# Reordering the fill products and slowing an inverse's steps in a one-core encoder layer, with the norm sum taken by 128 columns

## The chip, the core and the metric

The kernel runs on one core of a Trainium2 chip. The metric is the device time of one launch in microseconds (us), the median of several runs. One more run, taken with the hardware profiler on, gives the trace that is read here. TensorE is called PE in the profile's rows, its weight loads PEld, VectorE DVE, ScalarE ACT, GpSimd POOL; SP issues most DMAs.

## The reference

One encoder layer on two sequences of 256 tokens (T = 512 token columns in all, D = 1024), in float32:

```
h = RMSNorm(x)
proj = h @ w_in            # q|k|v of 8 heads, decay and beta logits, gates z, latents, 3 x 1024 merge gates
A: conv + SiLU on q, k, v; l2norm of q and k; gated delta rule in both directions; RMSNorm; * silu(z_gdn)
B: latent attention with rotary keys, 8 heads; * silu(z_mla)
C: cross-attention into 256 memory tokens, 4 heads; * silu(z_mem)
y = x + (gate0*(A @ w_br_gdn) + gate1*(B @ w_br_mla) + gate2*(C @ w_br_mem)) @ w_out, then RMSNorm
```

Branch A, per head and direction: within a chunk, a unit lower-triangular matrix (identity plus masked k k^T with decay and beta) is inverted; the inverse is applied to values and keys, a state is carried from chunk to chunk, and the output is normed over its 128 channels: `o * rsqrt(mean(o*o) + eps)`.

## The kernel before, in words

Every large product is made of 24 matmuls of 128x512: the weight block of 128 output rows and the activations are each split into a rounded part and a rest, and three of the four part products are summed over eight blocks of 128 (`gemm`, L257 to L278). A product needs its weights: a load that SP issues (L229), rounded by ScalarE (L241), the rest taken by VectorE (L244). It accumulates in a PSUM bank of the tag gm, of which `middle` has four, and holds it until its result is read out.

The work has three stages. `front` does the memory branch, the latents and the eight heads of branch B, with some products of branch A and of the gates put between. `middle` does the delta rule of branch A, head by head, and fills TensorE's free time with the remaining products. `back` does the last products and the output.

In `middle` the order of TensorE's instructions is written by a planner, `weave` (L1623). It keeps a clock of its own, `now`. Six chains are generators that yield a pair (cost on TensorE, time until the next step is due). When no chain's step is due, the planner takes one matmul from the fill list `self.fill` and moves its clock on by 0.217 us, which is the cost of a matmul that `gemm` yields. The chains are:

- `preps` (L1560): the block inverses of head group 0, then of group 1 (`gdn_prep`). Its 31 inverse steps (L900 to L906) are two VectorE instructions each, a multiply into `tm` (L903) and an add into `tt` (L905), on sizes 31 to 256 elements a partition; each step needs the one before. After them a reordering copy on GpSimd (L908), two transposes on VectorE (L911, L913) and seven copies on GpSimd (L922). For group 1 these copies wait until head 3 is in `self.started` (its `yp` products have been issued and 7.5 us of the planner's clock have passed). When they are done plus 4 us, heads 4 to 7 may be solved.
- `heads_in` (`gdn_in`): one head after the other, decay masks, the products `kk` of its keys and queries (L1010, two pairs a head, each of the four products three matmuls in a gm bank of its own), read out by VectorE into `ne` (L1020). A head begins when it is at most two ahead of the outputs and its values have been stored (`self.v_done`). 18 us of the planner's clock lie between its begin and its first `kk`.
- `lane(0)` and `lane(1)` (`gdn_solve`): the even and the odd heads, each a sequence of small products (`p`, `yp`, `u`, `xs`, `us`, `x`).
- `heads_out` (`gdn_out`): the output products `o`, the gate, and the norm's sum `so` (L1182), which adds, over the four blocks of 32 partitions, the sums of squares left there by a VectorE transpose and reduction; then a power on GpSimd (L1185), a transpose (L1188) and a store of the row `d_n`.
- `heads_norm` (`gdn_norm`): reads that row back and makes the head's operand `xg` of the branch product.

VectorE, ScalarE, GpSimd and SP are in-order queues; the order within them is set when the kernel is built, by a priority and a modelled readiness, not by hand. Chains get an earlier priority than fill (the inverse chain 100, a head's solve 2000).

The fill list (`plan`, L1425 to L1466) holds products of these kinds. A query or value product (`qkv_tile`) is read out by ScalarE into `cz` (L767), which frees its bank; then comes the convolution, four VectorE instructions (L776) and a last one (L778); `v_tokens` transposes a head's values on VectorE (L801) and stores them by four DMAs of SP. A gate product (`gate_tile`) is read out by one ScalarE instruction (L1248) and stored by one DMA of SP (L1254). A `z_tile` product is read out by ScalarE (L1220) and then by VectorE (L1221), and only the second frees its bank; those of branch C (here ze) also multiply by the attention output on GpSimd. `cz`, the gates' and the z tiles share two buffers of the tag ct. After the listed products come four loads of the branch C operands, eight branch C products with their gates, eight branch B products (bm, which need all operands `xa`), and the branch A products begun with the heads that are ready (`bg_begin`).

The norm's sum uses the constant `i32` (128 rows by 32 columns, a one where row mod 32 equals the column) as weights. In the constant tile the columns of `anc`, `trf`, `trb` and `i32` lie next to each other, 32 each.

Of the kernel before, what the change touches and what calls it, by code (L numbers as in the profile page):

```python
# [10 lines left out]
ALU = mybir.AluOpType  # L11
# [6 lines left out]
EPS = 1e-6  # L18
# [49 lines left out]
def _consts():  # L68
    t = np.arange(P)
    b = t // 32  # L70
    same = b[:, None] == b[None, :]
    le = t[:, None] <= t[None, :]
    ge = t[:, None] >= t[None, :]
    z, o = np.zeros((P, P)), np.ones((P, P))
    a8 = np.arange(8)
    anc = np.zeros((P, 2, 2, 8))
    for tb in range(2):
        tg = tb * P + t
        anc[:, 0, tb] = tg[:, None] >= 32 * a8[None]
        anc[:, 1, tb] = tg[:, None] < 32 * (a8[None] + 1)  # L80
    i32 = np.arange(32)
    m = (t % 32)[:, None]
    parts = [
        ("id", np.eye(P)),
        ("anc", anc.reshape(P, 32)),
        ("trf", m <= i32), ("trb", m >= i32), ("i32", m == i32),
        ("ngf", np.where(i32 > m, 0.0, NEG)), ("ngb", np.where(i32 < m, 0.0, NEG)),
        ("one", np.ones((P, 1))), ("hf", np.full((P, 4), -0.5)), ("ph", np.full((P, 16), 0.5)),
    ]
    off, c = {}, 0  # L90
    for n, a in parts:
        off[n] = (c, c + a.shape[1])
        c += a.shape[1]
    sums = [same, same & le, same & ge, z, le, o, o, ge, z]
    return (np.concatenate([a.astype(np.float32) for _, a in parts], 1), off,
            np.concatenate([a.astype(np.float32) for a in sums], 1))


_CST, _OFF, _SUM = _consts()
# [82 lines left out]
class Layer:  # L182
# [36 lines left out]
    def c(self, n):  # L219
        lo, hi = _OFF[n]  # L220
        return self.cst[:, lo:hi]
# [587 lines left out]
    def gdn_prep(self, g):  # L809
# [4 lines left out]
        nc, c = self.nc, self.c  # L814
# [85 lines left out]
        for i in range(31):  # L900
            n, m = 31 - i, i + 1
            t3 = tms[:, i % 4, 0:n * m].rearrange("p (a b) -> p a b", a=n)
            nc.vector.tensor_tensor(t3, xx[:, m:, i:i + 1].to_broadcast([P, n, m]),  # L903
                                    tt[:, i:i + 1, 0:m].to_broadcast([P, n, m]), op=ALU.mult)
            nc.vector.tensor_tensor(tt[:, m:, 0:m], tt[:, m:, 0:m], t3, op=ALU.add)  # L905
            yield 0.0, 1.2  # L906
        ts = self.pb.tile([P, 32, 32], F32, tag="blk", bufs=3, name=f"ts{g}")
        nc.gpsimd.tensor_copy(out=ts, in_=tt.rearrange("p r c -> p c r"))  # L908
        yield 0.0, 7.0
# [234 lines left out]
    def gdn_out(self, hh):  # L1144

        nc, pg, c = self.nc, self.pg, self.c
        par, kq = hh % 2, self.kq[hh]
        (na, es, vt), ub = self.hd[hh], self.ub[hh]

        op = self.ps_ms(par, f"o{hh}")  # L1150
        o3 = op.rearrange("p (s t) -> p s t", s=2)
        for s in range(2):
            n = 0
            for d in range(2):
                for cp in range(2):
                    if cp == 0:
                        out, rhs = o3[:, s], es[:, d, s, 0:256]
                    else:
                        lo = 128 * (1 - d)
                        out, rhs = o3[:, s, lo:lo + 128], es[:, d, s, 256:384]  # L1160
                    nc.tensor.matmul(out, ub[:, d, s, cp], rhs, start=n == 0, stop=n == 3)  # L1161
                    n += 1
            yield 1.3, 0.0

        og = self.ta(f"og{hh}")
        nc.sync.dma_start(og, self.d_z[:, hh])
        self.out = hh + 1
        nc.vector.scalar_tensor_tensor(og, op, self.gg, og, ALU.mult, ALU.mult)
        sq = self.tb(f"sq{hh}")
        nc.scalar.activation(sq, op, AF.Square)  # L1170
        with self.behind():
            nc.scalar.activation(kq[:, :, 1], kq[:, :, 1], AF.Square, scale=0.064)
        s3 = sq.rearrange("p (s t) -> p s t", s=2)
        nc.vector.tensor_tensor(s3, s3, kq[:, :, 1], op=ALU.add)
        st = self.tb(f"st{hh}")
        red = self.rr[:, 16:32]
        with self.behind():
            nc.vector.transpose(out=st, in_=sq)
            nc.vector.tensor_reduce(red, st.rearrange("p (j i) -> p j i", i=32), axis=AX.X, op=ALU.add)
        yield 0.0, 13 if hh == 7 else 12  # L1180
        ssp = self.ps_ms(par, f"so{hh}")
        nc.tensor.matmul(ssp[0:32, 0:16], c("i32"), red, start=True, stop=True)  # L1182
        rr = self.rr[0:32, 0:16]
        nc.vector.tensor_scalar(rr, ssp[0:32, 0:16], 1.0 / 128, 128 * EPS * EPS, ALU.mult, ALU.add)  # L1184
        nc.gpsimd.tensor_tensor(rr, rr, c("hf")[0:32, 0:1].to_broadcast([32, 16]), op=ALU.pow)  # L1185
        yield 0.25, 2.0 if hh == 7 else 4.0
        with self.behind():
            nc.vector.transpose(out=self.rt[0:32], in_=self.rr[0:32])  # L1188
        nc.sync.dma_start(self.d_n[hh].rearrange("(j i) -> j i", i=32), self.rt[0:16])
        self.og[hh] = og, self.now + 8.0  # L1190

    def keep(self, i):
# [244 lines left out]
    def plan(self):  # L1437

        self.kq, self.xg, self.merged = {}, {}, [None] * 8
        self.cn, self.now, self.prep_on = {}, 0.0, False  # L1440
        self.v_done, self.k_done, self.z_done = set(), set(), set()
        self.fill = []
        def qv(h):
            return [(self.qkv_tile, h, 1), (self.qkv_tile, h, 2)]

        k = [(self.qkv_tile, h, 0) for h in range(8)]
        vt = [(self.v_tokens, h) for h in range(8)]
        self.xe_split, self.begun, self.k_at, self.prep_steps = False, {}, 0.0, 0
        self.xe, self.xa, self.xa_at, self.xa_raw, A = [], [None] * 8, {}, {}, self.A
        xa = [(f, n) for n in range(5) for f in (self.load_xa, self.split_xa)]  # L1450
        g = [(self.gate_tile, j, d) for j in (0, 1) for d in range(8)]
        z = [(self.z_tile, C_ZG + h, self.d_z[:, h]) for h in range(8)]
        ze = [(self.z_tile, C_ZE + h, self.d_xm[:, h], self.d_om[:, h]) for h in range(4)]
        be = [(self.branch_mem, d) for d in range(8)]
        xe = [(self.load_xe, f) for f in range(4)]

        self.fill += g[0:1] + k[0:1] + g[1:2] + k[1:4] + qv(0) + vt[0:1] + qv(1) + vt[1:2] + g[2:3] + qv(2) + vt[2:3] + g[3:4] + qv(3) + vt[3:4] + g[4:6]

        self.fill += k[4:5] + g[6:7] + k[5:6] + g[7:8] + k[6:7] + g[8:9] + k[7:8] + z[0:1] + g[9:10] + z[1:2]
        self.fill += qv(4) + g[10:11] + z[2:3] + ze[0:1] + vt[4:5] + qv(5) + g[11:12] + z[3:4] + ze[1:2] + vt[5:6] + qv(6)  # L1460
        self.fill += g[12:13] + z[4:5] + ze[2:3] + vt[6:7] + qv(7) + g[13:14] + z[5:6] + ze[3:4] + vt[7:8] + g[14:15]
        self.fill += z[6:7] + xe + g[15:16] + z[7:8] + [(self.split_x, self.xe)]
        self.fill += xa + be
        self.fill += [(self.branch, 1, d, self.xa, A["w8"][C_BM:], "bm") for d in range(8)]
        self.fill += [(self.bg_begin, d) for d in range(4)]
# [253 lines left out]
```

## Time and profile before

| | |
|---|---|
| median of 3 runs | 806.63 us (807.34, 803.73, 806.63) |
| the profiled execution | 803.84 us, of which the traced span is 801.9 us |
| granted TensorE clock, mean | 0.997 |
| share of the chain that ended last | PE 87%, DVE 7%, ACT 2%, others 1% or less |
| DMA | 118.18 MB, mean 147 GB/s |

A row of the timeline gives start and length in us from the span's start, engine, line, operation, result and operands, shape and count; a bracket is the idle time of the engine before it and what ended it. Matmuls overlap: a 128x512 matmul lasts 0.38 us in the rows, while the next starts 0.216 us after it, so TensorE's pace is read from starts, not from lengths. A row of the windows gives a stretch, then for PE, PEld, DVE, ACT and POOL the busy time and number of instructions, then the granted clock, the share of the DMA engines and GB/s. A row of the groups gives what is one kind of instruction, its count, then busy time and mean length in ns, then the idle time just before.

### The profile page before, as it was taken

The page shows a single profiled execution, that of the slowest core. Times are in us where ns is not written, and L with a number is a line of the kernel's source. Part 1 is how long each engine was busy: PE and PEld are TensorE (multiplying, and loading weights), DVE is VectorE, ACT ScalarE, POOL GpSimd, SP SyncE. Part 2 cuts the span into 40 slices and gives each one's busy share as a digit, 9 for nine tenths or more (in the row PEclk, how much of TensorE's full clock was granted, in tenths as well). Part 3 has the DMA queues.
Part 4 walks back from the last instruction along what each step waited for, and adds up shares of the span by engine and source line. Part 5 has one row for each costly group of instructions (what it writes and reads, how often), then busy time and mean ns, then how long its engine had stood idle before and what let it go on. Part 6 is the DMA issues. An engine that isn't in the chain of part 4 may idle for free.

```text
span 801.9 us, 13065 instructions
## 1 busy us (share of the span) xinstructions
PE 789.5 (98%) x4774; PEld 692.6 (86%) x4774; DVE 582.2 (73%) x974; ACT 446.7 (56%) x894; POOL 168.2 (21%) x135
## 2 busy tenths in 40 slices
PE   8999999999999999999999989999999999999996
PEld 7888898889898889988888878888888888888886
DVE  7886358788699999578699999784564666465643
ACT  6755455556565556646766657664956463322332
POOL 0200111000010002073230336531412013333312
PEclk9999999999999999999999999999999999999999
DMA  9522222732427525445434454656553557554532
GB/s 328 171 78 101 92 84 72 246 105 83 113 62 225 164 96 155 138 140 169 130 116 132 119 151 150 188 168 170 174 158 108 178 169 256 171 191 157 177 106 105
DMA packets 68911, 118.18 MB, mean 147 GB/s; under 512 B 23664, under 2 KB 31344, under 8 KB 68848
## 3 DMA queue, kind: packets, MB, share of 16 engines
q1 hardware_dynamic: 67552, 115.03, 45.7%
q10 hardware_dynamic: 1296, 2.33, 0.8%
q8 instruction: 37, 0.61, 0.3%
q14 instruction: 26, 0.21, 0.1%
HBM read 98.24 MB, written 19.09 MB: 146 GB/s over the span
## 4 chain that ended last, share of the span: by engine, by line
PE 87%; DVE 7%; ACT 2%; DMA 1%; issue 1%; POOL 1%; SPq 0%; POOLq 0%; ACTq 0%; DVEq 0%
PE gm_qkv L276 14%; PE gm_g L276 14%; PE gm_z L276 5%; PE gm_za L276 5%; PE gm_bm L276 5%; PE y L1342 5%; PE gm_be L276 3%; PE gm_qm L276 3%; PE gm_km L276 3%; PE gm_bg L276 3%; PE vm L427 3%; PE o L1161 2%; PE gm_bg L1309 2%; PE s_a L330 2%; PE kk L1010 2%; PE gm_qn L276 2%
## 5 line engine op out<-in xcount | busy, mean ns | idle before, releaser
L776 DVE SCALAR_TENSOR_TENSOR kq<-cz,prm,kq 128x510 f32<-128x510 f32 (+1 forms) x64 | 53.7, 840 | 1.7 <-ACT kq L769 1.0
L276 PE MATMUL gm_qkv<-hh,wh_qkv 128*128 128x512 f32 x192 | 48.8, 389 | 2.8 <-DVE tm L903 2.7
L276 PE MATMUL gm_g<-hh,wl_g 128*128 128x512 f32 x192 | 49.0, 385 | 0.0
L276 PE MATMUL gm_qkv<-hl,wh_qkv 128*128 128x512 f32 x192 | 49.0, 389 | 0.0
L276 PE MATMUL gm_g<-hl,wh_g 128*128 128x512 f32 x192 | 47.8, 383 | 0.0
L276 PE MATMUL gm_g<-hh,wh_g 128*128 128x512 f32 x192 | 47.7, 384 | 0.0
L276 PE MATMUL gm_qkv<-hh,wl_qkv 128*128 128x512 f32 x192 | 47.0, 382 | 0.0
L244 DVE TENSOR_TENSOR wl_g<-wr_g,wh_g 128x1024 fp32r<-128x1024 f32 x24 | 30.0, 1252 | 20.9 <-ACT wh_g L241 10.9
L1284 POOL TENSOR_TENSOR mg<-mg,lg 128x512 f32<-128x512 f32 x16 | 28.5, 1788 | 74.8 <-DVE lg L1283 72.7
L276 PEld LDWEIGHTS gm_qkv<-hh,wh_qkv 128*128 128x128 f32 x192 | 35.7, 191 | 8.6 <-issue 3.1
L241 ACT ACTIVATE wh_g<-wr_g 128x1024 fp32r<-128x1024 f32 x24 | 25.3, 1052 | 31.1 <-PE gm_g L276 13.5
L276 PEld LDWEIGHTS gm_qkv<-hl,wh_qkv 128*128 128x128 f32 x192 | 36.4, 193 | 5.1
L1020 DVE SCALAR_TENSOR_TENSOR ne<-e,cc,kk 128x512 f32<-128x512 f32 (+1 forms) x64 | 35.5, 610 | 6.4 <-PE kk L1010 3.7
L276 PEld LDWEIGHTS gm_qkv<-hh,wl_qkv 128*128 128x128 f32 x192 | 35.8, 189 | 4.8
L276 PEld LDWEIGHTS gm_g<-hl,wh_g 128*128 128x128 f32 x192 | 35.7, 189 | 4.7
L276 PEld LDWEIGHTS gm_g<-hh,wh_g 128*128 128x128 f32 x192 | 35.5, 189 | 4.9
L276 PEld LDWEIGHTS gm_g<-hh,wl_g 128*128 128x128 f32 x192 | 35.3, 189 | 4.6
L1185 POOL TENSOR_TENSOR rr<-rr,cst 32x16 f32<-32x16 f32 x8 | 26.0, 3246 | 58.8 <-DVE rr L1184 58.8
L244 DVE TENSOR_TENSOR wl_qkv<-wr_qkv,wh_qkv 128x1024 fp32r<-128x1024 f32 x24 | 31.0, 1292 | 10.0 <-ACT wh_qkv L241 4.9
L1342 PE MATMUL y<-wh_wo,mh 128*128 128x512 f32 (+1 forms) x144 | 37.7, 356 | 0.0
L1024 POOL TENSOR_TENSOR vs<-vs,ns 128x512 f32<-128x512 f32 x8 | 8.4, 1046 | 126.1 <-DVE rs_a L347 85.2
L967 POOL TENSOR_SCALAR_AFFINE_SELECT e<-e 128x256 f32<-128x256 f32 x32 | 20.5, 666 | 65.6 <-DMA e<-d_r 39.8
(458 smaller groups left out, 2209.5 us busy)
## 6 DMA issues: line engine op xcount, KB each, us to landing
wr_g<-in_w_dram SPq DMA_DIRECT2D x24, 512.0 KB, 4.2
wr_qkv<-in_w_dram SPq DMA_DIRECT2D x24, 512.0 KB, 3.5
e<-d_r SPq DMA_DIRECT2D x64, 96.0 KB, 3.3
wr_z<-in_w_dram SPq DMA_DIRECT2D x12, 512.0 KB, 4.0
d_g<-gt_g SPq DMA_DIRECT2D x16, 256.0 KB, 2.3
wr_za<-in_w_dram SPq DMA_DIRECT2D x8, 512.0 KB, 3.7
lg<-d_g SPq DMA_DIRECT2D x16, 256.0 KB, 3.7
wr_bm<-in_w_dram SPq DMA_DIRECT2D x8, 512.0 KB, 3.7
```

Source lines behind the costliest of these rows:

```text
L241: self.wround = nc.scalar.activation(hi[:, :n], raw[:, :n], AF.Copy).ins
L244: self.wsplit = nc.vector.tensor_tensor(lo[:, :n], raw[:, :n], hi[:, :n].bitcast(F32), op=ALU.subtract).ins
L276: nc.tensor.matmul(pairs(ps[:m]), a[:, k * m:(k + 1) * m], turns(xs[k][j]), start=n == 0, stop=n == 3 * nk - 1)
L330: nc.tensor.matmul(pairs(sp[:, qb * 256:(qb + 1) * 256]), a, turns(b), start=j == 0, stop=j == n - 1)
L427: nc.tensor.matmul(pairs(vps[tb]), ms[k][a][:, t], turns(b[:, :512]), start=k == 0 and i == 0, stop=k == 7 and i == 2)
L776: nc.vector.scalar_tensor_tensor(ys, zs, self.cw[:, f, m:m + 1], ys, ALU.mult, ALU.add)
L967: self.nc.gpsimd.affine_select(out=e[:, :, r], in_=e[:, :, r], pattern=[[0, 2], [sg, 128]], compare_op=ALU.is_ge, fill=NEG, base=0, channe ...
L1010: nc.tensor.matmul(pairs(ps), a[:, k], turns(b), start=i == 0, stop=i == 2)
L1020: nev = nc.vector.scalar_tensor_tensor(ne[:, :, d, s, r], es[d][:, s, r].unsqueeze(1).to_broadcast([P, 2, n]), cc[:, d, w:w + 1], kin, ALU ...
L1185: nc.gpsimd.tensor_tensor(rr, rr, c("hf")[0:32, 0:1].to_broadcast([32, 16]), op=ALU.pow)
L1284: nc.gpsimd.tensor_tensor(self.merged[d], self.merged[d], gt, op=ALU.add)
L1342: nc.tensor.matmul(pairs(ps), xs[2 * j + q][a][:, t], turns(b[:, q * 512:(q + 1) * 512])[:, c0 // 2:c1 // 2], start=j == 0 and n == 0, sto ...
```

## The change

```
             nc.vector.tensor_tensor(tt[:, m:, 0:m], tt[:, m:, 0:m], t3, op=ALU.add)
-            yield 0.0, 1.2
+            yield 0.0, 2.4 if g else 1.2
...
         ssp = self.ps_ms(par, f"so{hh}")
-        nc.tensor.matmul(ssp[0:32, 0:16], c("i32"), red, start=True, stop=True)
-        rr = self.rr[0:32, 0:16]
-        nc.vector.tensor_scalar(rr, ssp[0:32, 0:16], 1.0 / 128, 128 * EPS * EPS, ALU.mult, ALU.add)
-        nc.gpsimd.tensor_tensor(rr, rr, c("hf")[0:32, 0:1].to_broadcast([32, 16]), op=ALU.pow)
+        last = slice(96, 128)
+        nc.tensor.matmul(ssp[:, 0:16], self.cst[:, _OFF["anc"][0]:_OFF["i32"][1]], red, start=True, stop=True)
+        rr = self.rr[last, 0:16]
+        nc.vector.tensor_scalar(rr, ssp[last, 0:16], 1.0 / 128, 128 * EPS * EPS, ALU.mult, ALU.add)
+        nc.gpsimd.tensor_tensor(rr, rr, c("hf")[last, 0:1].to_broadcast([32, 16]), op=ALU.pow)
         yield 0.25, 2.0 if hh == 7 else 4.0
         with self.behind():
-            nc.vector.transpose(out=self.rt[0:32], in_=self.rr[0:32])
-        nc.sync.dma_start(self.d_n[hh].rearrange("(j i) -> j i", i=32), self.rt[0:16])
+            nc.vector.transpose(out=self.rt[last], in_=self.rr[last])
+        nc.sync.dma_start(self.d_n[hh].rearrange("(j i) -> j i", i=32), self.rt[96:112])
...
-        self.fill += qv(4) + g[10:11] + z[2:3] + ze[0:1] + vt[4:5] + qv(5) + g[11:12] + z[3:4] + ze[1:2] + vt[5:6] + qv(6)
-        self.fill += g[12:13] + z[4:5] + ze[2:3] + vt[6:7] + qv(7) + g[13:14] + z[5:6] + ze[3:4] + vt[7:8] + g[14:15]
+        self.fill += qv(4) + g[10:12] + z[2:3] + ze[0:1] + vt[4:5] + g[12:13] + qv(5) + g[13:14] + z[3:4] + ze[1:2] + vt[5:6]
+        self.fill += g[14:15] + z[4:5] + qv(6) + ze[2:3] + z[5:6] + vt[6:7] + qv(7) + ze[3:4] + vt[7:8]
         self.fill += z[6:7] + xe + g[15:16] + z[7:8] + [(self.split_x, self.xe)]
```

It has three parts. The steps of the second group's inverse (g = 1) are due every 2.4 us of the planner's clock and not every 1.2. The weights of the norm's sum are the 128 constant columns that end with `i32`, so that the sum stands in the last 32 of 128 result rows; what follows works on partitions 96 to 127. And of the 24 fill products from the queries of head 4 on, the order changes (Q and V are query and value products of a head, g, z and ze as above; numbers in the first line are places):

```
place   1  2  3   4   5   6   7   8  9  10  11  12  13  14 15  16 17 18  19 20 21  22 23  24
before  Q4 V4 g10 z2  ze0 Q5  V5  g11 z3 ze1 Q6 V6  g12 z4 ze2 Q7 V7 g13 z5 ze3 g14 z6 g15 z7
after   Q4 V4 g10 g11 z2  ze0 g12 Q5 V5 g13 z3 ze1 g14 z4 Q6  V6 ze2 z5 Q7 V7 ze3 z6 g15 z7
```

The value transposes and stores of heads 5, 6 and 7 stand behind places 10, 15 and 20 before, and behind 12, 18 and 21 after.

## Prediction

> **What bounds the kernel now.** I read the page's first part, then TensorE in stretches, then the timeline around the one stretch that is worse than the others, then VectorE's groups there. The page says who is busy:
>
> ```profile
> PE 789.5 (98%) x4774; PEld 692.6 (86%) x4774; DVE 582.2 (73%) x974; ACT 446.7 (56%) x894; POOL 168.2 (21%) x135
> ```
>
> TensorE is busy all the time, so only its idle time, its slow matmuls and its own work can shrink. Two windows views follow, the first with its edges at the starts of places 1, 8, 11 and 13 of the fill list, the second around the start of place 11 (queries of head 6).
>
> ```profile
> 402.48:451.93 49.45, 49.45 (x343) 43.22 (x342) 48.59 (x94) 28.35 (x62) 10.62 (x11) 1.00 0.49 140
> 451.93:475.02 23.09, 20.35 (x133) 17.06 (x132) 21.90 (x46) 19.16 (x46) 8.95 (x7) 1.00 0.35 92
> 475.02:492.98 17.96, 17.96 (x114) 15.49 (x115) 16.46 (x28) 8.67 (x21) 7.94 (x8) 0.90 0.67 203
> ...
> 472.00:475.00 3.00, 0.28 (x2) 0.01 (x1) 2.86 (x7) 0.92 (x2) 1.04 (x1) 1.00 0.81 102
> 476.00:479.00 3.00, 3.00 (x9) 2.38 (x8) 3.00 (x6) 0.00 (x0) 1.77 (x1) 0.51 0.84 219
> ```
>
> VectorE is 48.59 of 49.45 us busy, then 21.90 of 23.09. At the end of that, TensorE works 0.28 of 3 us, and right after it its granted clock is 0.51. What it waits for is in the timeline:
>
> ```profile
> 457.49 0.81 PE L276 MATMUL gm_g<-hh,wl_g 128*128 128x512 f32 x3
> 458.14 0.38 PE L276 MATMUL gm_z<-hh,wh_z 128*128 128x512 f32 x1
> ...
> 464.06 0.68 PE L276 MATMUL gm_z<-hh,wl_z 128*128 128x512 f32 x2
> ...
> 466.60 2.87 ACT L975 ACTIVATE e<-e,ngcl 128x256 f32<-128x256 f32 x8
> 469.50 0.60 ACT L1220 ACTIVATE zt_z<-gm_z 128x512 f32<-128x512 f32 x1
> 471.17 1.11 PE L276 MATMUL gm_z<-hh,wl_z 128*128 128x512 f32 x4
> 472.86 1.14 DVE L903 TENSOR_TENSOR tm<-xx,tt 128x87 f32<-128x87 f32 x1
> 474.19 0.68 DVE L1221 SCALAR_TENSOR_TENSOR zt_z<-zt_z,gm_z 128x512 f32<-128x512 f32 x1
> 475.02 2.76 PE L276 MATMUL gm_qkv<-hh,wh_qkv 128*128 128x512 f32 x8 [2.74 <-DVE tm L903]
> 477.57 2.18 PE L276 MATMUL gm_qkv<-hl,wh_qkv 128*128 128x512 f32 x5
> 479.59 0.38 PE L1010 MATMUL kk<-kh 128*128 128x512 f32 x1
> ```
>
> The first two rows give TensorE's pace: three matmuls start between 457.49 and 458.14, one each 0.216 us. Product z3 ended at 464.7. ScalarE read it at 469.50, behind eight exponentials; VectorE's half, which frees the bank, came at 474.19, behind inverse steps among others. It ends at 474.87, and 0.15 us later place 11 begins. The row names `tm`, but place 11 reads nothing of it; the bank of z3 is the one that fits. So this is an eviction that was late because VectorE had a queue, and inverse steps go ahead in it. Their groups between 400 and 476, beside those of the convolutions:
>
> ```profile
> L905 DVE TENSOR_TENSOR tt<-tt,tm 128x31 f32<-128x31 f32 (+15 forms) x31 | 12.8, 413 | 0.5
> L903 DVE TENSOR_TENSOR tm<-xx,tt 128x31 f32<-128x31 f32 (+15 forms) x31 | 11.7, 376 | 0.4
> L776 DVE SCALAR_TENSOR_TENSOR kq<-cz,prm,kq 128x510 f32<-128x510 f32 (+1 forms) x8 | 6.0, 755 | 0.0
> L778 DVE SCALAR_TENSOR_TENSOR kq<-cz,kq 128x512 f32<-128x512 f32 x2 | 1.9, 926 | 0.0
> L801 DVE STREAM_TRANSPOSE vt<-vf 128x512 f32<-128x512 f32 x2 | 1.4, 696 | 0.0
> ...
> L903 DVE TENSOR_TENSOR tm<-xx,tt x31: 195/358/1139, 415.8 to 475.3; 128x31 f32<-128x31 f32 x2, 128x60 f32<-128x60 f32 x2, 128x87 f32<-128x87 f32 x2, 128x112 f32<-128x112 f32 x2
> ```
>
> 31 steps take 12.8 + 11.7 = 24.5 us of VectorE, spread over 415.8 to 475.7: 1.93 us a step, where the planner had asked for 1.2. They run as fast as they can.
>
> **Part 1, the order and the inverse's pace.** A query product costs VectorE (6.0 + 1.9) / 2 = 3.95 us of convolution; a value product about the same plus a transpose, 4.65; a gate none of this (all have the weight split). Places 1 to 7 held four such products before and hold two after, so 8.6 us of VectorE's work is asked for later; they come back at places 8 and 9. By place 11 the sum is then nearly the old one, so the gain isn't less work but who waits. Just ahead of place 11 stood z3 and ze1, freed by VectorE; now V5 and g13 stand there, freed by one ScalarE copy each. The inverse steps, due 2.4 us apart, are now issued among the readouts and no longer ahead of all of them. I take the stall as gone.
>
> Its price: the last four matmuls of ze1 start at 471.17 and at 0.216 us each leave room for the next product at 472.03; in the row, 1.11 us long for four, one of them starts 0.09 late, which makes 472.12. It starts at 475.02: 2.9 us. From there 13 matmuls take until 479.59, 4.57 us in place of 13 x 0.216 = 2.81: 1.7 us at half clock. Together 4.6 us. Bounds: nothing is gained if an equal stall comes elsewhere; no more than 4.6 can come from here.
>
> The Trainium skill ("TensorE: Matmul & The Clock Gate", section "What's actually happening") says that the clock falls to half after an idle window of about 3.4 us. The idle here is 2.74 us and the clock fell to 0.51 all the same; by the rule's length alone the 1.7 us would not be part of the stall and the sum below would be 799.8. The row decides, and the rule gets no chance of its own.
>
> What moves with the products: a gate brings one ScalarE readout and one SP store of 256 KB forward; Q and V take three ScalarE instructions each and, for V, four SP stores back. SP's weight loads stand far ahead:
>
> ```profile
> 472.02 0.67 SPq L229 DMA_DIRECT2D wr_g<-in_w_dram  x1
> ```
>
> That load is for place 13, which starts at 492.98: 21 us of cover, so a store that holds SP some us costs nothing; without that cover it would stop TensorE for as long. The values come later: head 5's store moves from behind place 10 to behind place 12 (475.02 to 492.98), head 6's from 15 to 18, head 7's from 20 to 21. Twelve places took 402.48 to 492.98, 7.5 us each, which puts the ends of 18 and 21 near 538 and 561. A head's first `kk` marks when it was let in, 18 us before:
>
> ```profile
> 544.01 1.29 PE kk L1010 x6
> ...
> 578.25 1.29 PE kk L1010 x6
> ...
> 620.11 1.29 PE kk L1010 x6
> ```
>
> Heads 5, 6 and 7 thus begin at about 526, 560 and 602, after 493, 538 and 561: no head is held, and the smallest margin is 22 us, so the lateness costs nothing.
>
> The inverse's end can hold heads 4 to 7. These rows give the place:
>
> ```profile
> 400.29 1.30 PE L855 MATMUL kd<-kq 128*32 128x32 f32 x128
> ...
> 491.05 5.25 POOL L922 COPY t<-o 32x512 f32<-32x512 f32 x4
> 494.58 0.45 PE L1087 MATMUL yp<-y,p1s 32*32 32x32 f32 x32
> ...
> 530.30 0.45 PE L1062 MATMUL p<-t,ne 32*32 32x32 f32 x32
> ```
>
> The planner issues the steps from the end of `kd` (401.5 in trace time). With 2.4 us a step, about 0.2 lost at each while it finishes a matmul or another chain's products (an estimate from costs of 0.217 and 0.3 to 1.3), they are issued until 401.5 + 31 x 2.6 = 482, and 7 + 4 us later, at 493, the copies could be. They wait for head 3 in any case: its `yp` at 494.58, less the stall of 4.6, plus 0.3 + 7.5, is 498. About 5 us to spare, so head 4's `p` keeps its place. On VectorE the steps may run late by as much as they were before: the end was 475.7, and the first copies that use it began at 491.05.
>
> **Part 2, the norm's sum.** The rows that follow 458.14 above, at one of its eight places, then rows around a product `u` of four matmuls on full weights, then two groups of weight loads:
>
> ```profile
> 458.45 0.23 PE L1182 MATMUL so<-rr,cst 128*32 128x16 f32 x2
> 458.61 0.92 PE L276 MATMUL gm_z<-hh,wh_z 128*128 128x512 f32 x3
> ...
> 421.82 0.38 PE L276 MATMUL gm_z<-hh,wh_z 128*128 128x512 f32 x1
> 422.03 0.61 PE L1118 MATMUL u<-vs,y 128*128 128x128 f32 x4
> 422.40 0.89 PE L276 MATMUL gm_z<-hh,wh_z 128*128 128x512 f32 x3
> ...
> L1182 PEld LDWEIGHTS so<-rr,cst 128*32 128x32 f32 x16 | 1.1, 108 | 2.7 <-issue 1.3 <-DVE rr L1179 0.7 <-PE gm_g L276 0.3
> L297 PEld LDWEIGHTS ss_mem<-cst,mem 128*128 128x128 f32 x8 | 1.2, 191 | 0.1
> ```
>
> Three matmuls without a break last 0.81 us (457.49). The start of `so` comes 0.31 after 458.14, 0.09 too late; `so` takes 0.16; the three after it last 0.92, 0.11 too long: 0.36 us. The four of `u` take 0.37 + 0.08 = 0.45, 0.11 each, with no wait ahead. Two matmuls on full weights then cost 0.22; eight heads gain 8 x 0.14 = 1.1 us. Bounds: as dear as `u`, 0.45, loses 0.7; half of 0.22 gains 2.0. I take 1.1, the row of equal weights. What follows (power, transpose, store) works on as many elements as before: nothing.
>
> The Trainium skill speaks against it ("TensorE: Matmul & The Clock Gate", section "Step-by-step: what each phase is for"): the time of a weight load grows with the number of columns. The two load groups agree, 108 and 191 ns.
>
> **Sum.** 803.84 - 2.9 - 1.7 - 1.1 = 798.1 us for a profiled execution. That execution lies 2.8 below the median of 806.63 and within the runs shown (803.73 to 807.34); by the median it is 800.9. I predict the middle, **799.5**, against 805.2 on the same scale (0.7% less). About 0.5%, 4.0 us, is what a measurement of this kernel can tell from no change.
>
> **Rivals.** *The stall moves.* z3 is now place 11, and if banks return in their order of use, g14 at place 13 needs its bank one place, 7.5 us, after z3 ends. In the rows z3's readout was over 474.87 - 464.7 = 10.1 us after its end. If ScalarE's exponentials and the inverse's tail make it as late again, TensorE waits 10.1 - 7.5 = 2.6 us and loses the 1.7 again: 805.2 - 4.6 + 4.3 - 1.1 = 803.8. For it: VectorE's total by place 11 hardly falls. Against it: in 475 to 493 two products with convolutions have left.
>
> *The order does nothing.* VectorE sets the pace (1.93 us a step), so asking for 2.4 may change nothing and another eviction holds place 11. Only the norm's 1.1 is left: 804.1.
>
> *The norm's sum gets dearer.* If the longer loads are not hidden, 2 x (191 - 108) ns x 8 = 1.3 us is lost in place of 1.1 gained: 801.9 with the stall gone. Against it: `u` with the same loads runs at 0.11 a matmul.
>
> *Slower: the inverse comes too late.* Past the 5 us of margin, each us moves head 4, then head 7, then the operand of the last branch B parts:
>
> ```profile
> L256 DVE SCALAR_TENSOR_TENSOR xa<-xa x4: 686/688/689, 656.6 to 667.1; 128x512 fp32r<-128x512 f32 x4
> ...
> 665.80 3.24 PE gm_bm L276 x15
> ```
>
> The last `xa` ends at 667.8, and the matmuls that need it come after 15 others, at 669.0: 1.2 us of slack, and no other product is left to fill with. With d us beyond the margin TensorE idles d - 1.2 and loses 1.7 of clock; less the gain of 5.7, it is slower by 4.0 from d = 9.2, that is from 3.1 us a step. At d = 10 it is 810. Against it: the planner would have to lose 0.7 at each step, not 0.2.
>
> **How the numbers follow.** Forecast 0.54; stall moves 0.24; order does nothing 0.08; norm dearer 0.04; too late 0.10. Faster by over 0.5%: the forecast less 0.02 for residues, 0.52. Within: 0.02 + 0.24 + 0.08 + 0.04 = 0.38. Slower: 0.10. The range takes in the first four cases: below, 799.5 less 0.9 (the better bound of the norm) and less 2 of scatter between runs, 796.5; above, 804.1 and the same scatter, 806. The forecast's own range is 796.5 to 802.
>
> **What would show it.** Right: no idle of TensorE over 1 us between 400 and 500, a granted clock of 1.00 there, the last `tt` of group 1 near 480, `so` in the form 128x16 on 128 columns with 0.22 us lost, head 4's `p` about 5 us earlier than 530.3. Wrong: an idle stretch at place 13 ahead of g14 (the stall moved), one at the same place 11 with a clock near 0.5 (the order does nothing), or one ahead of a bm product near 665 (too late).

## The result, and the profile after

| | before | after |
|---|---|---|
| median of 5 runs | 805.29 us (803.73 to 807.34) | 799.09 us (798.62 to 799.44) |
| ratio, 95% interval | | 0.9922 (0.9905 to 0.994) |
| the profiled execution | 803.84 us, span 801.9 | 799.43 us, span 797.7 |

The change makes the kernel 0.78% faster; 799.5 us had been forecast. The two profiled executions differ by 4.4 us, the medians by 6.2. The first difference is traced below, the second only in part. One profiled execution further on, the first of the kernel with two products swapped, was disturbed (2137 us) and is not used.

First the page's line of busy times of after, then three rows of its windows view; the first has its edges at the starts of places 8 and 11, as before.

```profile
PE 787.3 (99%) x4774; PEld 693.3 (87%) x4774; DVE 582.9 (73%) x974; ACT 447.5 (56%) x894; POOL 167.1 (21%) x135
```

```profile
451.93:472.70 20.77, 20.04 (x133) 17.28 (x131) 19.89 (x42) 14.26 (x33) 9.23 (x6) 1.00 0.33 102
472.00:475.00 3.00, 2.30 (x11) 2.03 (x12) 3.00 (x5) 2.92 (x7) 0.00 (x0) 1.00 0.59 191
476.00:479.00 3.00, 2.84 (x15) 2.60 (x16) 3.00 (x6) 0.14 (x1) 1.21 (x1) 1.00 0.63 192
```

The third column is TensorE, the fifth VectorE. Where TensorE had worked 0.28 of 3 us it works 2.30, and the clock after it is 1.00 in place of 0.51. VectorE is as full as ever: 19.89 of 20.77 us. The timeline of after around place 11:

```profile
468.30 0.19 DVE L905 TENSOR_TENSOR tt<-tt,tm 128x31 f32<-128x31 f32 x1
...
469.15 2.88 ACT L975 ACTIVATE e<-e,ngcl 128x256 f32<-128x256 f32 x8
...
470.86 1.11 PE L276 MATMUL gm_g<-hh,wl_g 128*128 128x512 f32 x4
471.97 1.23 DVE L911 STREAM_TRANSPOSE o<-ts 128x1024 f32<-128x1024 f32 x1
472.05 0.60 ACT L767 ACTIVATE cz<-gm_qkv 128x512 f32<-128x512 f32 x1
...
472.70 1.99 PE L276 MATMUL gm_z<-hh,wh_z 128*128 128x512 f32 x8 [0.74 <-ACT cz L767]
...
474.26 0.70 DVE L776 SCALAR_TENSOR_TENSOR vf<-cz,prm,vf 128x510 f32<-128x510 f32 x1
...
474.88 2.18 DVE L1020 SCALAR_TENSOR_TENSOR ne<-e,cc,kk 128x512 f32<-128x512 f32 x4
...
476.16 0.45 PE L1010 MATMUL kk<-kh 128*128 128x512 f32 x1 [0.39 <-DVE ne L1020]
```

Place 11 (now z3) could start at 470.86 + 4 x 0.216 + 0.09 = 471.8 and starts at 472.70: 0.9 us lost, to ScalarE's readout of V5, which stood behind eight exponentials, as z3's readout did before. A little later `kk` loses 0.55 us more to a readout by VectorE. So 2.9 us of idle and 1.7 of half clock have become 1.45 us of idle at full clock: 3.15 us gained, not 4.6.

Not all of the 2.9 us was queue. The multiply at 472.86 in the prediction's rows (128x87) took 1.14 us, where the same one takes 0.26 in after. GpSimd ran a multiply of its own beside it, 1.04 us long from 472.85 (L1024). The second profile of before and e3, both below, have an inverse instruction of 1.03 and 1.15 us near there, each beside that GpSimd multiply. So some 0.9 us of the wait goes with it; no run tests this by itself.

The norm's sum in after, in the timeline and in the groups of weight loads:

```profile
458.14 0.38 PE L276 MATMUL gm_qkv<-hh,wh_qkv 128*128 128x512 f32 x1
458.36 0.29 PE L1183 MATMUL so<-rr,cst 128*128 128x16 f32 x2
458.50 1.33 PE L276 MATMUL gm_qkv<-hh,wh_qkv 128*128 128x512 f32 x5
```

```profile
L1183 PEld LDWEIGHTS so<-rr,cst 128*128 128x128 f32 x16 | 2.9, 190 | 1.0 <-DVE rr L1179 0.7
```

`so` now starts 0.22 us after the matmul ahead of it, that is at once, takes 0.14 us, and the five after it last 1.33 where 4 x 0.216 + 0.38 = 1.24 would be unbroken: 0.23 us in place of 0.36, for all that each weight load now takes 190 ns and not 108. Seven of the eight places gain about 0.14 us, as here. At the eighth (640.3 us before, 635.9 after), `so` waits for VectorE's reduction both times and nothing is gained. That makes 0.9 us in all.

3.15 + 0.9 and 0.23 us at place 16 (below) make 4.3. Place 1 starts at 402.48 us before and at 402.51 after, so nothing ahead of it counts, and the spans differ by 4.2.

### The profile page after: what moved, and what is told of

It reads as the page before. It is cut to its first block, busy times and chain, and to the rows that moved or that the text cites. A ratio compares the mean times of both kernels' runs of the same rounds, so it can differ in the third digit from the quotient of the medians.

```text
span 797.7 us, 13066 instructions
## 1 busy us (share of the span) xinstructions
PE 787.3 (99%) x4774; PEld 693.3 (87%) x4774; DVE 582.9 (73%) x974; ACT 447.5 (56%) x894; POOL 167.1 (21%) x135
## 4 chain that ended last, share of the span: by engine, by line
PE 93%; DVE 4%; ACT 1%; issue 1%; DMA 0%; POOL 0%; POOLq 0%; ACTq 0%; DVEq 0%
PE gm_g L276 14%; PE gm_qkv L276 14%; PE gm_z L276 8%; PE gm_za L276 5%; PE gm_bm L276 5%; PE y L1343 5%; PE vm L427 3%; PE gm_be L276 3%; PE o L1161 3%; PE gm_qm L276 3%; PE gm_km L276 3%; PE gm_bg L276 3%; PE kk L1010 3%; PE gm_bg L1310 2%; PE s_a L330 2%; PE gm_qn L276 2%
## 5 line engine op out<-in xcount | busy, mean ns | idle before, releaser
L276 PE MATMUL gm_qkv<-hh,wh_qkv 128*128 128x512 f32 x192 | 46.8, 381 | 0.0
L241 ACT ACTIVATE wh_qkv<-wr_qkv 128x1024 fp32r<-128x1024 f32 x24 | 25.3, 1055 | 17.7 <-PE gm_z L276 5.0
L1186 POOL TENSOR_TENSOR rr<-rr,cst 32x16 f32<-32x16 f32 x8 | 24.0, 3001 | 48.1 <-DVE rr L1185 47.9
```

The source lines that it names most:

```text
L241: self.wround = nc.scalar.activation(hi[:, :n], raw[:, :n], AF.Copy).ins
L276: nc.tensor.matmul(pairs(ps[:m]), a[:, k * m:(k + 1) * m], turns(xs[k][j]), start=n == 0, stop=n == 3 * nk - 1)
L1186: nc.gpsimd.tensor_tensor(rr, rr, c("hf")[last, 0:1].to_broadcast([32, 16]), op=ALU.pow)
```

## The experiments

"Place" is a place in the list of 24 fill products above, counted in the order of the kernel in question. Ratios are to the kernel before, run on the same chip.

**One part at a time.** Four kernels carry the change's parts alone or without one:

```
e1  before, with only the norm's sum changed
e2  before, with only the two fill lines changed
e3  before, with only  yield 0.0, 2.4 if g else 1.2
e4  after, with  yield 0.0, 1.2  put back
```

> The norm's sum on 128 columns alone, order and pace as before. Every theory of the sum has it cost 0.22 us a head in place of 0.36, so 1.1 us in all: a ratio near 0.9986 and the stall ahead of place 11 as before, 2.9 us and half clock after it. If the longer weight loads were not hidden it would be 1.3 us slower (1.0016). If the stall depends on the order in which the other queues were built, it may be any size from 0 to 3 us, and then the ratio says nothing of the sum; the rows around the sum do.

> The order of the fill products alone; inverse steps due every 1.2 us, norm's sum as before. Theory (the order): place 11 waits for a bank that ScalarE frees, so the stall shrinks to below 1 us and the clock stays at 1.00: 3 to 4.6 us less than before (ratio 0.994 to 0.996). Rival (the pace): inverse steps due at 1.2 us go ahead of the readouts as before, the stall stays at 2 to 3 us and the time within 1 us of before.

> Inverse steps of the second group due every 2.4 us, all else as before. Theory (the order): the steps run as early as VectorE lets them whatever the planner asks, z3 and ze1 still stand ahead of place 11, the stall stays at 2 to 3 us, time within 1 us of before. Rival (the pace): the steps no longer go ahead of z3's readout, the stall falls below 1 us and the time by 3 to 4.6 us.

> The whole change but for the pace (inverse steps due every 1.2 us). Theory (the order): as the whole change within 1 us, 799 to 800 us where before has 805, stall below 1 us. Rival (the pace): stall of 2 to 3 us with half clock after it, so only the norm's 1.1 us is gained, 804 us.

| | median, us | ratio, 95% interval |
|---|---|---|
| e1, norm alone | 804.40 | 0.9989 (0.9978 to 1.0) |
| e2, order alone | 799.64 | 0.9932 (0.9917 to 0.9948) |
| e3, pace alone | 805.42 | 1.0006 (0.9993 to 1.002) |
| e4, order and norm | 799.47 | 0.9928 (0.9913 to 0.9943) |

The order alone brings nearly all. The pace alone brings nothing, and the whole change with it (0.9922) can't be told from e4 without it. TensorE's timeline around place 11, first of e2, then of e3:

```profile
470.54 1.11 PE L276 MATMUL gm_g<-hh,wl_g 128*128 128x512 f32 x4
471.93 1.99 PE L276 MATMUL gm_z<-hh,wh_z 128*128 128x512 f32 x8 [0.28 <-ACT cz L767]
```

```profile
471.16 1.11 PE L276 MATMUL gm_z<-hh,wl_z 128*128 128x512 f32 x4
475.00 3.22 PE L276 MATMUL gm_qkv<-hh,wh_qkv 128*128 128x512 f32 x8 [2.73 <-DVE tm L903]
```

With the order alone, place 11 loses 0.4 us; with the pace alone, 475.00 - 472.1 = 2.9 us, the very stall of before. Why the pace does nothing is in the row of the inverse's multiplies, whose second pair of numbers is the start of the first and of the last one; e2 (due every 1.2 us), e3 (2.4), then after (2.4):

```profile
L903 DVE TENSOR_TENSOR tm<-xx,tt x31: 136/358/511, 415.5 to 467.4; 128x31 f32<-128x31 f32 x2, 128x60 f32<-128x60 f32 x2, 128x87 f32<-128x87 f32 x2, 128x112 f32<-128x112 f32 x2
```

```profile
L903 DVE TENSOR_TENSOR tm<-xx,tt x31: 191/353/1360, 415.3 to 475.3; 128x31 f32<-128x31 f32 x2, 128x60 f32<-128x60 f32 x2, 128x87 f32<-128x87 f32 x2, 128x112 f32<-128x112 f32 x2
```

```profile
L903 DVE TENSOR_TENSOR tm<-xx,tt x31: 191/357/425, 415.8 to 468.1; 128x31 f32<-128x31 f32 x2, 128x60 f32<-128x60 f32 x2, 128x87 f32<-128x87 f32 x2, 128x112 f32<-128x112 f32 x2
```

The last step starts at 467.4 or 468.1 with the new order and at 475.3 with the old one, whatever is asked for. This fits a planner that fixes TensorE's order, while on VectorE the steps are placed as soon as they are ready.

VectorE could end them earlier because it had less else to do. Its groups for the convolutions of values between 400 and 476, of before and then of after:

```profile
L776 DVE SCALAR_TENSOR_TENSOR vf<-cz,prm,vf 128x510 f32<-128x510 f32 (+1 forms) x8 | 5.9, 738 | 0.0
```

```profile
L776 DVE SCALAR_TENSOR_TENSOR vf<-cz,prm,vf 128x510 f32<-128x510 f32 (+1 forms) x5 | 3.7, 731 | 0.0
```

Before, V4's and V5's eight instructions were all done by place 11. In after only V4's four were; V5's first one, the fifth here, starts at 474.26, behind place 11. With V5's last instruction and its transpose, 0.7 us each, 4.3 us of VectorE's work now come later.

e1's rows at the norm's sum are those of after (0.23 us). Its ratio stands for 0.9 us, as those rows give, but the interval reaches to no change, so the timed runs alone don't show it. e1's waits were its own: place 11 waited 1.9 us and not 2.9, with no half clock after it, and a second place waited too, place 16 (Q7, behind z4 and ze2). At place 11 GpSimd's multiply began behind the inverse steps of 128x87, and VectorE's half of z3 started at 473.12, where before it had been 474.19:

```profile
473.06 1.04 POOL L1024 TENSOR_TENSOR vs<-vs,ns 128x512 f32<-128x512 f32 x1 [4.15 <-DVE tm L903]
473.12 0.68 DVE L1222 SCALAR_TENSOR_TENSOR zt_z<-zt_z,gm_z 128x512 f32<-128x512 f32 x1
...
508.59 1.89 PE L276 MATMUL gm_z<-hh,wl_z 128*128 128x512 f32 x8
512.59 1.97 PE L276 MATMUL gm_qkv<-hh,wh_qkv 128*128 128x512 f32 x8 [2.11 <-DVE zt_z L1222]
```

Eight matmuls from 508.59 end their turn at 510.32; Q7 starts at 512.59, 2.3 us late.

**Before, once more.** That led to a second profile of the unchanged kernel.

> The kernel before, unchanged, for a second profile of it: does the stall at place 11 differ from run to run? If the scatter of before (802.8 to 807.9) comes from it, the stall here is not 2.9 us, and another stall stands behind z products ahead of place 16; if not, place 11 shows 2.9 again and the span differs elsewhere.

It took 806.36 us. Its timeline at place 11 and at place 16:

```profile
473.25 1.11 PE L276 MATMUL gm_z<-hh,wl_z 128*128 128x512 f32 x4
476.99 1.97 PE L276 MATMUL gm_qkv<-hh,wh_qkv 128*128 128x512 f32 x8 [2.63 <-DVE tm L903]
478.79 1.24 PE L276 MATMUL gm_qkv<-hl,wh_qkv 128*128 128x512 f32 x5
479.87 0.38 PE L1010 MATMUL kk<-kh 128*128 128x512 f32 x1
...
511.55 1.89 PE L276 MATMUL gm_z<-hh,wl_z 128*128 128x512 f32 x8
515.37 1.97 PE L276 MATMUL gm_qkv<-hh,wh_qkv 128*128 128x512 f32 x8 [1.94 <-DVE zt_z L1221]
```

And the same place 16 in the first profile of before:

```profile
511.26 1.89 PE L276 MATMUL gm_z<-hh,wl_z 128*128 128x512 f32 x8
513.22 1.97 PE L276 MATMUL gm_qkv<-hh,wh_qkv 128*128 128x512 f32 x8
```

The same program loses 2.1 us there in one execution and 0.23 in the other. At place 11 both lose about 2.8 to 2.9, but in this one the 13 matmuls that follow take 2.88 us, full clock, and not 4.57. So the kernel before has two places that wait for a z product, and the second one, and the half clock behind the first, come and go. In the five profiles with the old order around place 16 and all of the old work, it loses 0.2 (before), 0.4 (e3), 1.5 (e9, below), 2.1 (e7) and 2.3 us (e1). In the profiles of after, e2, e4 and the two kernels below that are neighbours of the change, place 16 (V6, behind Q6) loses nothing.

But this is not what makes the second execution 2.5 us longer than the first: what it loses more at place 16 it gains by the clock. A third wait differs, in `front`, far ahead of all that the change touches. Its rows in the second profile, then in the first:

```profile
272.30 0.89 PE L276 MATMUL gm_qn<-qlh,wh_qn 128*128 128x512 f32 x3 [2.52 <-DVE kn L254]
```

```profile
270.69 0.89 PE L276 MATMUL gm_qn<-qlh,wh_qn 128*128 128x512 f32 x3 [0.29 <-DVE kn L254]
```

It costs 2.7 us in one and 0.5 in the other, and in the profiles of other kernels from 0 (e2, e3) to 1.1 (e1) and 1.6 (e4). So two things can widen the 4.4 us of one pair of profiles to the 6.2 of the medians. One is the wait at place 16, which the change removes. The other is scatter that has nothing to do with it: five runs of before cover 803.7 to 807.3 and five of after 798.6 to 799.4, but six runs of e4, with the same order, 798.4 to 801.5. How much each gives was not separated.

**Which is it: the bank of one product, or VectorE's backlog?** Two fill products exchanged, then the same kernel once more:

```
-  ... + qv(5) + g[11:12] + z[3:4] + ze[1:2] + ...
+  ... + qv(5) + z[3:4] + g[11:12] + ze[1:2] + ...
```

> Before, with two fill products exchanged: place 8 is z3 and place 9 is g11, so that VectorE's work asked for by place 11 is the same. Theory (the bank of the product two places ahead): z3 gets one place, about 6 us, more to be read out, and what stands two places ahead of place 11 is a gate, which ScalarE frees; the stall of 2.9 us at place 11 falls below 1 us and the half clock with it: 3 to 4.6 us less in the profile, ratio 0.995 to 0.997. Rival (VectorE's total): the work is the same, so a stall of 2 to 3 us stays at place 11 or right behind it, ratio 0.999 to 1.001.

> The exchange of g11 and z3 once more, for a profile. Its timed runs came to 0.9986 of before, between the two theories. Theory (late readout, whichever product suffers): the stall at place 11 is below 1 us, and the stall at place 16, behind z4 and ze2, is there as in the second profile of before, 2 us. Rival (VectorE's total): a stall of 2 to 3 us at place 11, 12 or at the products kk beside them.

The timed runs gave 0.9986 (0.9966 to 1.0005), 803.51 us, which can't be told from before. The timeline of its repetition, the second label:

```profile
472.79 1.24 PE L276 MATMUL gm_qkv<-hl,wh_qkv 128*128 128x512 f32 x5
475.46 0.45 PE L1010 MATMUL kk<-kh 128*128 128x512 f32 x1 [1.44 <-DVE tt L905]
...
476.62 0.45 PE L1010 MATMUL kk<-kh 128*128 128x512 f32 x1 [0.27 <-DVE ne L1020]
...
507.80 1.89 PE L276 MATMUL gm_z<-hh,wl_z 128*128 128x512 f32 x8
511.05 1.32 PE L276 MATMUL gm_qkv<-hh,wh_qkv 128*128 128x512 f32 x5 [1.36 <-DVE zt_z L1221]
```

Place 11 no longer waits, as the theory of the bank has it; but the next products that want a bank, `kk`, wait 1.6 and 0.4 us for VectorE, as the rival has it. Place 16 waits 1.5 us. Taking one late readout out of the way uncovers the next one.

The same from another side: z3's bank is freed by ScalarE at once, order and VectorE's work as before.

```
         th = self.ct("zt_" + name)
+        if o is None:
+            zc = self.ta("zc_" + name)
+            with self.tc.high_priority(offset=60):
+                nc.scalar.activation(zc, ps, AF.Copy)
+            ps = zc
         self.silu2(th, ps)
```

> Before, but a z product of branch A is copied out of PSUM by ScalarE at once, and its tanh and VectorE's product read the copy; VectorE's work and the order are unchanged, ScalarE has 8 copies of 0.6 us more. Theory (the bank waits for VectorE's late instruction): the stalls at places 11 and 16 fall below 1 us, 3 to 5 us less, ratio 0.994 to 0.996. Rival (VectorE's total, by whatever way): stalls of 2 us or more stay, at these places or others, ratio 0.998 or above.

It took 810.94 us, ratio 1.0064 (1.0041 to 1.0088). The theory missed; the rival's stalls "at these places or others" came, but neither had expected a slower kernel. The timeline at place 11 and, later, at a head's solve:

```profile
473.98 1.24 PE L276 MATMUL gm_qkv<-hl,wh_qkv 128*128 128x512 f32 x5
476.90 0.45 PE L1010 MATMUL kk<-kh 128*128 128x512 f32 x1 [1.68 <-DVE ne L1020]
...
565.12 0.59 PE L276 MATMUL gm_g<-hh,wh_g 128*128 128x512 f32 x2
569.68 0.50 PE L1087 MATMUL yp<-y,p1s 32*32 32x32 f32 x32 [3.97 <-ACT p1s L1066]
```

Place 11 is free again and `kk` waits 1.8 us for VectorE again; place 16 waits 1.3 us, now for ScalarE's copy. The loss is elsewhere: TensorE stands 4 us at a head's solve for a ScalarE copy. The edit also takes a buffer that the heads' outputs share; which of the two, the copies or the buffer, made ScalarE late was not separated.

And VectorE's backlog taken away, order as before:

```
         for i in range(31):
+            if g and i >= 18:
+                yield 0.0, 1.2
+                continue
```

> Before, with the last 13 of 31 inverse steps of the second group left out (heads 4 to 7 then have an unfinished inverse, so the output is not the reference's; it is there for its time alone). It takes some 8 us of VectorE's work out of the 23 us ahead of place 11, order unchanged. Theory (z3 is read out late because VectorE has a queue): the stall at place 11 falls below 1 us, 3 to 4.6 us less in the profile. Rival (only the order of the bank's users counts): z3's bank is still late, the stall stays above 2 us.

800.89 us, 0.9962 (0.9942 to 0.9983). Place 11:

```profile
470.54 1.11 PE L276 MATMUL gm_z<-hh,wl_z 128*128 128x512 f32 x4
472.34 1.97 PE L276 MATMUL gm_qkv<-hh,wh_qkv 128*128 128x512 f32 x8 [0.69 <-DVE zt_z L1224]
```

0.86 us in place of 2.9, with z3 where it was. What is left is ScalarE's: it reads z3 from 470.88 to 471.47, behind its exponentials, and VectorE's half follows at 471.50 at once. So it is the backlog that makes VectorE's readouts late.

The new order does two things about it. It puts products that ScalarE frees (V5, g13) ahead of place 11 in place of z readouts, and it moves V5's convolution, 4.3 us, behind place 11. e9 has something like the first alone: place 11 is free, but `kk` pays 2.0 us. e8 has only less work for VectorE, and takes more of it away: 0.86 us are left at place 11. The change has both: 0.9 + 0.55 us. No run moves V5's convolution and nothing else.

**Two neighbours of the change.** The first moves g12 behind V5 (`qv(5) + g[12:14] + z[3:4]` after ze0), so that two gates stand ahead of z3:

> The whole change, with g12 moved from ahead of Q5 to behind V5 (places 7 to 10: Q5 V5 g12 g13). V5 then has two places in which ScalarE can read it out before place 11. Theory (what counts is that the product two places ahead has been read out): the 0.9 us left at place 11 go, 0.5 to 1 us less than the whole change, ratio to before 0.991. Rival (VectorE's load counts): two convolutions are asked for one place earlier, as before the change, and inverse steps stand beside them; place 11 waits 1 us or more, ratio 0.993 or above.

799.86 us, 0.9929 (0.9907 to 0.9951): not to be told from the change. Its timeline shows why, place 11 without a wait and `kk` with more:

```profile
474.56 1.24 PE L276 MATMUL gm_z<-hl,wh_z 128*128 128x512 f32 x5
476.61 0.45 PE L1010 MATMUL kk<-kh 128*128 128x512 f32 x1 [0.81 <-DVE ne L1020]
...
477.66 0.45 PE L1010 MATMUL kk<-kh 128*128 128x512 f32 x1 [0.16 <-DVE ne L1020]
```

The 0.9 + 0.55 us of after are 0.97 + 0.33 here. So the theory holds at place 11 and the rival in the total; V5's convolution is ahead of place 11 again, and the inverse's last multiply starts at 473.7.

The second neighbour sets the inverse's steps 3.0 us apart (`yield 0.0, 3.0 if g else 1.2`), past the margin that the prediction had worked out:

> The whole change, with inverse steps of the second group due every 3.0 us and not 2.4. Theory (the rival that the prediction called too late): with 0.2 us lost a step they are issued until 401.5 + 31 x 3.2 = 501, the copies could begin at 512 and head 3 would have let them at 498, so d = 14 us; head 4's p moves from 526 to about 540, products run out ahead of the last heads, TensorE idles 14 - 1.2 us and some of it at half clock: 799 + 13 to 15 = 812 to 814. Other view (the planner only orders, and VectorE runs the steps as early as it can): less than 3 us slower.

798.30 us (798.06 to 798.78), 0.9923 (0.99 to 0.9947): no slower at all. Head 4's and head 7's `p` and head 7's `o`, in after and then in e6:

```profile
526.50 0.45 PE L1062 MATMUL p<-t,ne 32*32 32x32 f32 x32
...
629.96 0.45 PE L1062 MATMUL p<-t,ne 32*32 32x32 f32 x32
...
692.90 1.36 PE L1161 MATMUL o<-ne,ub 128*128 128x256 f32 x7
```

```profile
537.83 0.45 PE L1062 MATMUL p<-t,ne 32*32 32x32 f32 x32
...
639.52 0.45 PE L1062 MATMUL p<-t,ne 32*32 32x32 f32 x32
...
694.47 1.91 PE L1161 MATMUL o<-ne,ub 128*128 128x256 f32 x10
```

The expectation missed. The planner did hold head 4 back, by 11.3 us (14 had been expected), and head 7 by 9.6. But head 7's solve then took 55 us and not 63, and its end is late by 1.6. This fits the planner's code, in which the clock jumps to the next due time when the fill list has nothing to offer, while no time passes on the chip; it was not traced step by step.

## Why the prediction was right, point by point

**The stall.** It was read as a late readout by VectorE that holds a bank, and taken as gone. That held in kind: the half clock is gone, 2.9 us became 0.9 with 0.55 beside it (e2 alone: 0.4 and 0.6). The term was 4.6 and measured 3.15 in the profiled pair; its 1.7 us of half clock are not in every execution of before (e7 has none). What stands ahead of place 11 (V5 and g13, freed by ScalarE) is borne out by e2 and e9. "By place 11 the sum is then nearly the old one, so the gain isn't less work but who waits" is so for what is asked for, and not for what is done: 4.3 us of V5's convolution and transpose had been done by place 11 before and come after it now. e8 and e9 show that both count. "No idle over 1 us" and a clock of 1.00 came as said.

**The pace.** "The inverse steps, due 2.4 us apart, are now issued among the readouts" is the step that failed. They were expected to end near 480 and ended at 468, earlier than before; e3 and e6 show that the pace neither gains nor, up to 3.0 us, loses. The row of 1.93 us a step, quoted as a sign that VectorE sets the pace, had said so; the rival that "the order does nothing" drew from it the wrong half: the pace does nothing, and the order alone gives a ratio of 0.9932 where the whole change gives 0.9922.

**The norm.** Seven of eight heads gain about 0.14 us each, as forecast from the row of `u`; the eighth waits for VectorE either way, so it is 0.9 us for 1.1. The weight loads did get longer (190 ns for 108), but not the path.

**What was costed at nothing.** Values of heads 5 to 7 later, stores of gates earlier: head 4's `p` is at 526.50, 3.8 us ahead of 530.30, which is the time gained by then, so no head was held.

**The number.** 799.5 against 799.09 rests partly on chance. The sum of 5.7 us was 1.3 too large for the profiled pair, and the medians moved by 0.5 more than it. In part this can be the kernel before's second such wait at place 16. It was not seen: its profile shows 0.23 us there, and e7 and e1 2.1 and 2.3. In part it can be scatter like that of the wait in `front`, which the prediction had in no term.

**The rivals.** The stall did move, as far as `kk` and not to place 13, and with 0.55 us and not 2.6. That the order does nothing is refuted by e2, the dearer norm by e1's rows. The inverse too late was wrong in its price: the margin was placed about right, and past it no time was lost.

## What to carry to other kernels

On an engine that is full, ask what stands in its queue when the bottleneck next needs something of it. Here readouts on which a bank hung went out of that position, and work that nothing waited for went behind it; the new order was worth 0.7%, with the same total of work in the kernel. One profile shows one execution of each wait: profile the same kernel twice before pricing a stall, and compare place by place. And a matmul on fewer weight columns than the rest of the stream was dearer here than one on all of them.

## What the runs showed of the hardware

TensorE's granted clock fell to half in three profiles, for 3.41 us each time: in before (from 476.05 to 479.46 us) behind an idle time of 2.74 us, in e3 behind 2.73, in e11 (from 569.96) behind 3.97. It did not fall behind 2.63 us in the second profile of before (13 matmuls in 2.88 us), nor behind 1.76 and 2.11 us in e1. The Trainium skill ("TensorE: Matmul & The Clock Gate", section "What's actually happening") says that the window of about 3.4 us runs freely. The traces agree: in each of the twelve profiles used here, the time between two changes of the granted clock is a whole number of steps of 3.413 us (in before 471.04 us from its rise to its fall, 138 steps; in e11 563.20 us, 165 steps).

Laid on these steps, the one just ahead of each fall holds 2.4 (before), 2.7 (e3) and 3.1 us (e11) in which no matmul ran. From the first rise to the last matmul, no other step of any profile holds more than 1.84 (the second profile of before). So in these runs the clock fell by how much of an idle time lay in one step, not by its length alone, and 2.4 us of a step were enough; where between 1.84 and 2.4 the limit lies is open.

A VectorE multiply of 128x87 took 1.14 us beside a GpSimd multiply of 1.04 us in before, and 0.25 us in e1 (at 472.67) with GpSimd idle. VectorE's half of z3, which takes one operand from PSUM, ran its usual 0.68 us in e1 beside that GpSimd multiply.

Two matmuls of 16 columns in the 128x32 form cost 0.36 us among matmuls of the full form, 0.09 of it ahead of them, where the same on 128 columns starts without a gap and costs 0.23.
